# Last heads of a gated recurrence reordered, more MLP strips opened ahead, on one Trainium2 core

## The chip, the cores and the metric

The kernel runs on one core of a Trainium2 chip. The core has five engines that run side by side, each through a queue of its own in order: PE (TensorE, the matrix multiplier, with PEld for its weight loads), DVE (VectorE), ACT (ScalarE), POOL (GpSimd) and SP (SyncE, which here only issues DMAs). They wait for each other through semaphores. The metric is the device time of one execution in microseconds (us), as the median of several runs.

## The reference

A decoder trunk of two layers on one sequence of 1024 tokens, 1024 channels wide, everything in float32. Each layer is a token mixer followed by a gated MLP with a causal convolution over three tokens, each added to the residual stream. Layer 0's mixer is a gated linear recurrence (eight heads, 128 channels each), layer 1's is a multi-head latent attention. What matters here, cut:

```python
def _chunk_gated_recurrence(q, k, v, log_f):    # S_t = diag(f_t) S_{t-1} + k_t v_t^T ; o_t = S_t^T q_t
...
def _hgrn2_mixer(h, w_in, lower_bound, out_norm, w_out):
    q, f, i, g = jnp.split(h @ w_in, 4, axis=-1)
    ...
    forget = lb + (1.0 - lb) * jax.nn.sigmoid(f)
    o = _chunk_gated_recurrence(heads(jax.nn.silu(q)), heads(1.0 - forget), heads(i), heads(jnp.log(forget)))
    o = _rmsnorm(o, out_norm) * jax.nn.silu(heads(g))
    return o.reshape(B, S, D_MODEL) @ w_out

def _conv_ffn(h, w_up, conv_w, conv_b, w_down):
    u = h @ w_up                                # 1024 -> 2 * 2816
    y = conv_b + sum(u_pad[:, j:j + S, :] * conv_w[j] for j in range(3))
    gate, up = jnp.split(y, 2, axis=-1)
    return (jax.nn.silu(gate) * up) @ w_down
```

Both mixer and MLP read an RMS-normalised x (each token divided by the root of its mean square, then scaled per channel).

## The kernel before

The residual stream x stays on the chip as two halves of the sequence, `xt[0]` and `xt[1]`, each 128 partitions x 8 tiles x 512 tokens. A float32 product is made of three matmuls: each operand is split into a rounded part (`hi`, ACT's cast, L126) and its rest (`lo`, a subtraction on DVE or POOL, L129), and hi·hi + hi·lo + lo·hi is summed (L145 to L147, and `product`, L243, whose matmuls are recorded as L247). Weights come by SP's DMAs into a raw buffer and are split the same way (`load_w`; `whi`, `wlo`; three buffers each).

**The recurrence (layer 0).** A unit is one head on one half of the sequence. `project` (L333) makes its gate F, K, Q, v and g by 48 matmuls of 512 columns and 96 of 256; `recur` (L380) runs six levels of scores (`sc`, L388), each scaled on DVE (Q, L399) and POOL (K, L401) and folded into a score matrix `SD` (L392, L411), then the outputs `po` (L433, L435) and the state (L438, L443). The sum of squares of `po` for the head's norm is taken by four ACT squares whose elementwise result goes to a scrap tile `junk` (L447), followed by a chain of small DVE operations on `ss`, `oy`, `oz` (L450, L451) and the scaling of g (L453). `flip` (L457) transposes g and splits it (`oh`, `ol`), `wout` (L466) multiplies by the output weights and adds eight results into x (L299). The list `units` (L472) sets the order: head by head, first half then second, but the last four are (6,0), (7,0), (6,1), (7,1) as (head, half). While a unit's recurrence runs, the next unit's projection and the former unit's `wout` fill PE. The weights of a head are loaded when the head changes from one unit to the next (L499), so heads 6 and 7 are loaded twice.

**The MLP's up phase.** It works in 22 strips of 128 hidden channels for gate and up. Each strip is a 2x2 block product (halves of the inner dimension, halves of the sequence) done with seven products of 12 matmuls in place of eight (84 matmuls of 128x512). Its operands are block sums: `first_half` (L274) normalises `xt[0]` and splits it into two operands (`bop`), `second_half` (L278) normalises `xt[1]`, forms four differences (L285) and splits five more. `normalize` (L261) is: save x by a DMA, squares of the eight tiles on ACT with the sums on POOL (k below 4) and DVE (`token_scale`, L200 to L214), a matmul that sums over partitions (L165), an inverse root of twelve small DVE operations (L149), two diagonal matrices (`dg`, L189), a broadcast matmul (L197), an ACT copy `rb` (L219), and eight DVE operations that scale x in place (L266).

Two of the seven products need only the first half. `open_strips` (L250) does these two ahead for the strips in `OPENED` (L237: 1, 3, ... 15, eight of them): 24 matmuls each, copied out by ACT (`part`, L258) and saved by a DMA. In the strip loop (L924) an opened strip reads the saved part back and runs the other five products (60 matmuls); an unopened one runs all 84 there (`combos`, L832, makes the sums of its weights on DVE).

**What sets the order.** The tile framework gives every operation a priority by its place in the program, and orders each engine's queue by priority and by when operands come; code in `tc.high_priority()` goes ahead. On the chip each queue runs in that fixed order. `first_half` is written after the last unit's recurrence (L502), ahead of the last `wout`; `second_half` and `open_strips` follow, then the strips. Pools of one or two buffers (two `ps_mm` banks in PSUM, one `SD`, one `junk`) tie the queues together. Layer 1 uses the same `normalize`, `first_half`, `open_strips` and strips behind the attention.

Of the kernel before, what the change touches and what calls it, by code (L numbers as in the profile page):

```python
# [9 lines left out]
F32 = mybir.dt.float32  # L10
# [9 lines left out]
P = 128  # L20
D = 1024
# [5 lines left out]
NFF = DFF // P  # L27
# [31 lines left out]
def trunk_kernel(ctx: ExitStack, tc: tile.TileContext, x, pos, par, gout, cst, msk, w_hin, w_hout,  # L59
                 w_min, w_qup, w_kvup, w_mout, w_up, w_down, out):  # L60
    nc = tc.nc
    pe, dve, act, pool = nc.tensor, nc.vector, nc.scalar, nc.gpsimd
# [55 lines left out]
    rope_t = const.tile([P, 2, HF], F32, name="rope_t")  # L118

    def pcol(name, i):  # L120
        c = PC[name] + i
        return prm[:, c:c + 1]
# [46 lines left out]
    def token_rstd(groups, n, extra=None, tag="misc", name="st_y", vname="st_v"):  # L169
        sums = token_sums(groups, tag)  # L170
        w = 4 * len(groups)
        v = tpool.tile([P, w], F32, tag=vname, name="st_v", bufs=2 if vname == "st_v" else 1)
        y = tpool.tile([P, w], F32, tag=name, name="st_y", bufs=2 if name == "st_y" else 1)
        z = tpool.tile([P, w], F32, tag="st_z", name="st_z")
        if extra is None:
            dve.tensor_scalar(out=v, in0=sums, scalar1=1.0 / n, scalar2=EPS, op0=ALU.mult, op1=ALU.add)
        else:
            dve.scalar_tensor_tensor(out=v, in0=sums, scalar=1.0 / n, in1=extra, op0=ALU.mult, op1=ALU.add)
        rsqrt(v, y, z)
        return (y, v) if vname != "st_v" else y  # L180
# [12 lines left out]
    def bcast(y, tag="misc", lo_eng=pool):  # L193
        dg = diag(y, lo_eng)
        ps = ps_misc(tag)
        for i in range(2):
            pe.matmul(ps, lhsT=ones_r, rhs=dg[:, i].rearrange("p a b -> p (a b)"), start=(i == 0), stop=(i == 1))  # L197
        return ps

    def token_scale(hf):  # L200
        acc = tpool.tile([P, HF], F32, tag="acc", name="acc", bufs=1)
        acc2 = tpool.tile([P, 2 * HF], F32, tag="diag", name="acc2", bufs=1)[:, 0:HF]
        act.activation(out=acc2, in_=xt[hf][:, 0, :], func=AF.Square)
        for k in range(1, KD):
            if k == 4:
                act.activation(out=acc, in_=xt[hf][:, k, :], func=AF.Square)
                continue
            sq = tpool.tile([P, HF], F32, tag="sq", name="sq")
            act.activation(out=sq, in_=xt[hf][:, k, :], func=AF.Square)
            if k < 4:  # L210
                pool.tensor_tensor(out=acc2, in0=acc2, in1=sq, op=ALU.add)
            else:
                dve.tensor_tensor(out=acc, in0=acc, in1=sq, op=ALU.add)
        dve.tensor_tensor(out=acc, in0=acc, in1=acc2, op=ALU.add)  # L214
        return token_rstd([[acc]], D, name=f"y{hf}", vname=f"v{hf}")

    def spread_scale(hf, y, lo_eng=pool):
        rb = tpool.tile([P, HF], F32, tag=f"rb{hf}", name="rb", bufs=1)
        act.copy(out=rb, in_=bcast(y, lo_eng=lo_eng))  # L219
        return rb  # L220
# [13 lines left out]

    KH = KD // 2
    LO, HI = slice(0, KH), slice(KH, KD)
    OPENED = tuple(range(1, 17, 2))  # L237
    L, R = slice(0, HF), slice(HF, S)

    def halves(t):  # L240
        return [[x[:, i * HF:(i + 1) * HF] for x in t] for i in range(2)]
# [8 lines left out]
    def open_strips(layer, h):  # L250
        b11, b21 = h
        for j in OPENED:
            a11, a12 = halves(load_w(w_up[layer][j], eng=dve))
# [6 lines left out]

    def normalize(hf, layer):  # L261
        nc.sync.dma_start(out=xs[hf], in_=xt[hf])
        rb = spread_scale(hf, token_scale(hf)[0], dve)
        for k in (0, 4, 1, 5, 2, 6, 3, 7):
            xk = xt[hf][:, k, :]
            dve.scalar_tensor_tensor(out=xk, in0=xk, scalar=pcol("ffn", 8 * layer + k), in1=rb,  # L266
                                     op0=ALU.mult, op1=ALU.mult)
# [34 lines left out]
    def hgrn(layer, h):  # L302
        with ExitStack() as st:
            tp = st.enter_context(tc.tile_pool(name="g_t", bufs=2))
            early = st.enter_context(tc.tile_pool(name="g_e", bufs=2))
            wv = st.enter_context(tc.tile_pool(name="g_wv", bufs=1))
# [73 lines left out]
            def recur(hd, hf, prj, state):  # L380
                Fg, K, q, Q, v, g = prj
# [9 lines left out]
                SD = tp.tile([P, 4, 64], F32, tag="SD", name="SD", bufs=1)  # L391
# [35 lines left out]
                act.copy(out=kT, in_=pT)  # L427
                po = ps.tile([P, 4, P], F32, tag="o", name="po")
                ss = tp.tile([P, 4], F32, tag="ss", name="ss")
                junk = tp.tile([P, P], F32, tag="junk", name="junk", bufs=1)  # L430
                for c in range(4):
                    first = state is None
                    pe.matmul(po[:, c, :], lhsT=ST[:, c, :], rhs=v[:, c, :], start=True, stop=first)  # L433
                    if not first:
                        pe.matmul(po[:, c, :], lhsT=Q[:, c * P:(c + 1) * P], rhs=state, start=False, stop=True)  # L435
                    if not (hf == 1 and c == 3):
                        pu = ps.tile([P, P], F32, tag="sc", name="pu", bufs=2)
                        pe.matmul(pu, lhsT=kT[:, c, :], rhs=v[:, c, :], start=True, stop=True)  # L438
                        ns = tp.tile([P, P], F32, tag=f"state{hd % 2}", name="state")
                        if first:  # L440
                            act.copy(out=ns, in_=pu)
                        else:
                            dve.scalar_tensor_tensor(out=ns, in0=state, scalar=tot[:, c:c + 1], in1=pu,  # L443
                                                     op0=ALU.mult, op1=ALU.add)
                        state = ns
                for c in range(4):
                    act.activation(out=junk, in_=po[:, c, :], func=AF.Square, accum_out=ss[:, c:c + 1])  # L447
                y = tp.tile([P, 4], F32, tag="oy", name="oy")
# [21 lines left out]
                    add_x(hf, d, p)  # L470

            units = [(hd, hf) for hd in range(HEADS) for hf in range(2)]  # L472
            units[-3], units[-2] = units[-2], units[-3]
            vg_first = []
            for i, tag in enumerate(("hh1", "hl1")):
                raw = hpool.tile([P, 1024], F32, tag=tag, name="vgraw", padded_shape=[P, KD * HF])
# [1 line left out]
                vg_first.append(raw)  # L478
            weights(0)
            nc.sync.dma_start(out=xt[1], in_=x[1])  # L480
            goutb = wv.tile([P, P], F32, tag="goutb", name="goutb")
            nc.sync.dma_start(out=goutb, in_=gout.partition_broadcast(P))
            nc.sync.dma_start(out=cs, in_=cst)
            mstage = tp.tile([P, len(LEVELS), 64], F32, tag="ST", name="mstage", bufs=1)
# [3 lines left out]
            h.append(norm_x(1, "mix", layer))  # L488
            states, wos = {}, {}
            for i, (hd, hf) in enumerate(units):  # L490
                if hf == 0:
                    wos[hd] = load_w(w_hout[hd], "wo", wop, 2)
                late = [(pend[0], pend[1], *flip(pend[2]))] if i else []
                g, states[hd] = recur(hd, hf, prj, states.get(hd))
                for w in late:
                    wout(*w)
                pend = (hf, wos[hd], g)
                if i + 1 < len(units):
                    if units[i + 1][0] != hd:  # L499
                        weights(units[i + 1][0])  # L500
                    prj = project(*units[i + 1])
                if i + 1 == len(units):  # L502
                    h2 = first_half(layer)
            wout(pend[0], pend[1], *flip(pend[2]))
            return h2
# [320 lines left out]
    def up_phase(layer, h, wfp, ps_up):  # L826
        with ExitStack() as st:
# [44 lines left out]
            def strip(j, prev):  # L872
                opened = j in OPENED
                c = combos(j, opened)
# [178 lines left out]
```

## Time and profile before

| | |
|---|---|
| median of 3 runs | 2605.51 us (2604.63 to 2606.7) |
| the profiled execution | 2608.18 us, span 2606.4 us, mean granted TensorE clock 0.982 |
| busy share of the span | PE 95%, PEld 78%, DVE 69%, ACT 39%, POOL 19% |
| last unit pair of the recurrence, (6,1) and (7,1) | 605 to 654 us, the rest of the mixer to 684 us |
| opened strips of layer 0 and the wait at their end | 684 to 733.5 us |
| DMA | 228 MB, mean 88 GB/s |

The span is divided by stage: the recurrence takes the first 654 us, the up phase of layer 0 follows to about 1360 us with its down phase, the attention ends near 1920 us, and the second MLP fills the rest. A row of the timeline gives the start, the duration, the engine, the source line, the operation, what it writes from what it reads with the shapes, and in brackets how long the engine was idle ahead of it and what released it. `(x4110)` counts instructions.

### The profile page before, as it was taken

The page shows a single profiled execution, that of the slowest core. Times are in us where ns is not written, and L with a number is a line of the kernel's source. Part 1 is how long each engine was busy: PE and PEld are TensorE (multiplying, and loading weights), DVE is VectorE, ACT ScalarE, POOL GpSimd, SP SyncE. Part 2 cuts the span into 40 slices and gives each one's busy share as a digit, 9 for nine tenths or more (in the row PEclk, how much of TensorE's full clock was granted, in tenths as well). Part 3 has the DMA queues.
Part 4 walks back from the last instruction along what each step waited for, and adds up shares of the span by engine and source line. Part 5 has one row for each costly group of instructions (what it writes and reads, how often), then busy time and mean ns, then how long its engine had stood idle before and what let it go on. Part 6 is the DMA issues. An engine that isn't in the chain of part 4 may idle for free.

```text
span 2606.4 us, 35442 instructions
## 1 busy us (share of the span) xinstructions
PE 2474.9 (95%) x13732; PEld 2043.3 (78%) x13732; DVE 1795.3 (69%) x3218; ACT 1026.1 (39%) x1697; POOL 504.7 (19%) x489
## 2 busy tenths in 40 slices
PE   7999999998889999999999999999879999999999
PEld 6888888887667778888888777777757777888887
DVE  7455565667778888774545887877878888875333
ACT  4322222232444444433433444444434444443322
POOL 4343333543000000000013444443400000000000
PEclk9999999999999999999999899999989999999999
DMA  3011100211323232264431000000033332226443
GB/s 145 34 41 41 33 33 25 74 59 56 117 97 117 105 107 90 95 226 154 137 115 57 9 17 17 17 25 9 33 123 123 110 109 101 97 88 223 153 169 119
DMA packets 67561, 228.21 MB, mean 88 GB/s; under 512 B 7616, under 2 KB 8000, under 8 KB 66240
## 3 DMA queue, kind: packets, MB, share of 16 engines
q1 hardware_dynamic: 67392, 225.94, 24.5%
q8 instruction: 108, 1.77, 0.3%
q14 instruction: 61, 0.50, 0.1%
HBM read 181.87 MB, written 44.04 MB: 87 GB/s over the span
## 4 chain that ended last, share of the span: by engine, by line
PE 77%; DVE 16%; ACT 3%; issue 2%; DMA 1%; POOL 0%; ACTq 0%; DVEq 0%; SPq 0%; POOLq 0%
PE ps_mm L247 18%; PE ps_up L247 8%; PE ps_up L946 7%; PE ps_mm L145 6%; PE ps_mm L147 6%; PE ps_mm L146 6%; PE ps_mm L946 5%; PE ps_wo L946 4%; PE ps_wo L247 3%; PE sc L388 2%; PE ps_misc L946 2%; DVE x L299 2%; PE sp L701 2%; PE ps_wo L145 1%; DMA wraw<-in_w_up_dram 1%
## 5 line engine op out<-in xcount | busy, mean ns | idle before, releaser
L126 ACT CAST whi<-wraw 128x1024 fp32r<-128x1024 f32 (+1 forms) x312 | 304.9, 991 | 564.1 <-PE ps_misc L946 240.9
L247 PE MATMUL ps_mm<-bop,whi 128*128 128x512 f32 x1536 | 485.3, 398 | 40.2 <-ACT bop L126 15.8
L129 DVE TENSOR_TENSOR wlo<-wraw,whi 128x1024 fp32r<-128x1024 f32 (+1 forms) x266 | 299.5, 1139 | 286.0 <-ACT whi L126 282.6
L247 PEld LDWEIGHTS ps_mm<-bop,whi 128*128 128x128 f32 x1536 | 290.3, 191 | 115.2 <-ACT bop L126 16.3
L247 PE MATMUL ps_mm<-bop,wlo 128*128 128x512 f32 x768 | 299.7, 395 | 0.9 <-DVE wlo L129 0.9
L866 DVE SCALAR_TENSOR_TENSOR x<-x,prm,x 128x1023 f32<-128x1023 f32 (+1 forms) x176 | 223.6, 1280 | 50.5 <-ACT x L863 49.5
L247 PE MATMUL ps_up<-bop,whi 128*128 128x512 f32 x704 | 221.6, 395 | 0.4 <-ACT whi L126 0.4
L247 PEld LDWEIGHTS ps_mm<-bop,wlo 128*128 128x128 f32 x768 | 146.2, 190 | 33.6 <-DVE wlo L129 1.4
L946 PE MATMUL ps_up<-ring,whi 128*128 128x512 f32 x528 | 159.8, 389 | 0.0
L247 PEld LDWEIGHTS ps_up<-bop,whi 128*128 128x128 f32 x704 | 132.0, 188 | 32.5 <-ACT whi L126 2.0
L129 POOL TENSOR_TENSOR wlo<-wraw,whi 128x1024 fp32r<-128x1024 f32 x46 | 113.2, 2463 | 219.3 <-ACT whi L126 219.3
L145 PE MATMUL ps_mm<-vgh,hh 128*128 128x256 f32 x512 | 145.1, 284 | 5.4 <-DVE q L355 5.4
L147 PE MATMUL ps_mm<-vgh,hl 128*128 128x256 f32 x512 | 145.0, 283 | 0.0
L146 PE MATMUL ps_mm<-vgl,hh 128*128 128x256 f32 x512 | 143.7, 281 | 0.0
L247 PE MATMUL ps_up<-bop,wlo 128*128 128x512 f32 x352 | 138.5, 394 | 0.0
L399 DVE TENSOR_TENSOR Q<-Q,tot 128x256 f32<-128x256 f32 x96 | 63.0, 656 | 103.7 <-PE sc L388 79.8
L863 ACT ACTIVATE x<-x,prm 128x1024 f32<-128x1024 f32 x88 | 109.5, 1244 | 62.0 <-DVE x L890 38.3
L701 PE MATMUL sp<-kk,qq 128*128 128x384 f32 (+4 forms) x480 | 112.1, 363 | 16.6 <-ACT pp L716 13.5
L849 DVE TENSOR_TENSOR wraw<-wraw 128x512 f32<-128x512 f32 x176 | 121.0, 688 | 2.1
L145 PE MATMUL ps_mm<-hh,whi 128*128 128x512 f32 x288 | 115.6, 402 | 2.5 <-DVE g L375 1.6
L401 POOL TENSOR_TENSOR K<-K,tot 128x256 f32<-128x256 f32 x96 | 78.4, 816 | 192.8 <-PE sc L388 124.1
L946 PEld LDWEIGHTS ps_up<-ring,whi 128*128 128x128 f32 x528 | 99.1, 188 | 20.6
(302 smaller groups left out, 5689.6 us busy)
## 6 DMA issues: line engine op xcount, KB each, us to landing
wraw<-in_w_up_dram SPq DMA_DIRECT2D x104, 512.0 KB, 3.7
wraw<-in_w_down_dram SPq DMA_DIRECT2D x88, 512.0 KB, 3.5
act_spill<-x SPq DMA_DIRECT2D x44, 512.0 KB, 2.6
araw<-act_spill SPq DMA_DIRECT2D x88, 256.0 KB, 3.6
wraw<-in_w_hin_dram SPq DMA_DIRECT2D x38, 512.0 KB, 3.5
x_spill<-x SPq DMA_DIRECT2D x4, 2048.0 KB, 6.7
open_spill<-part SPq DMA_DIRECT2D x32, 256.0 KB, 2.3
x<-open_spill SPq DMA_DIRECT2D x16, 512.0 KB, 3.2
```

The costliest lines, as they stand in the source:

```text
L126: act.copy(out=hi, in_=src)
L129: lo_eng.tensor_tensor(out=lo, in0=src, in1=hi.bitcast(F32), op=ALU.subtract)
L145: pe.matmul(ps, lhsT=lh, rhs=rh, start=(i == 0), stop=False)
L146: pe.matmul(ps, lhsT=lh, rhs=rl, start=False, stop=False)
L147: pe.matmul(ps, lhsT=ll, rhs=rh, start=False, stop=(i == n - 1))
L247: pe.matmul(p, lhsT=a[l][:, ks], rhs=b[:, r, k, :], start=first and k == 0 and n == 0, stop=k == KH - 1 and n == 2, skip_group_check=not f ...
L401: pool.tensor_tensor(out=Kv[:, :, 0, :], in0=Kv[:, :, 0, :], in1=tv[:, :, 1:2].broadcast_to([P, nb, m]), op=ALU.mult)
L701: pe.matmul(sp[:, 0:n], lhsT=qq[:, a, qs], rhs=kk[:, c, cl], start=(i == 0), stop=last)
L849: dve.tensor_tensor(out=o, in0=p, in1=q, op=op)
L863: act.activation(out=y, in_=u, func=AF.Identity, scale=cw(2, ff), bias=pcol("cb", layer * 44 + ff))
L866: dve.scalar_tensor_tensor(out=y[:, i:S], in0=u[:, 0:S - i], scalar=cw(2 - i, ff), in1=y[:, i:S], op0=ALU.mult, op1=ALU.add)
L946: pe.matmul(acc[d], lhsT=w[l][:, d * P:(d + 1) * P], rhs=a[:, r], start=j == 0 and n == 0, stop=j == NFF - 1 and n == 2)
```

## The change

Five edits. (1) The last six units run as (5,0), (6,0), (7,0), (5,1), (6,1), (7,1), so heads 5, 6 and 7 are loaded twice, the state has three buffers, and the output weights are loaded again too. `first_half` is written after unit (5,1), two units ahead of the end. (2) `OPENED` holds 1, 3, ... 21: eleven strips. (3) In `normalize` the squares keep their priority, and everything from the partition sum to `rb` goes ahead in priority. (4) The scrap tile of the squares is no longer a tile of its own, but the front of `SD`. (5) `goutb` (the head norm's gain) lies in `rope_t`, which is filled only later.

```diff
-    def token_scale(hf):
+    def token_squares(hf):
...
-        return token_rstd([[acc]], D, name=f"y{hf}", vname=f"v{hf}")
+        return acc
+
+    def token_scale(hf):
+        return token_rstd([[token_squares(hf)]], D, name=f"y{hf}", vname=f"v{hf}")
...
-    OPENED = tuple(range(1, 17, 2))
+    OPENED = tuple(range(1, NFF, 2))
...
     def normalize(hf, layer):
         nc.sync.dma_start(out=xs[hf], in_=xt[hf])
-        rb = spread_scale(hf, token_scale(hf)[0], dve)
+        acc = token_squares(hf)
+        with tc.high_priority():
+            rb = spread_scale(hf, token_rstd([[acc]], D, name=f"y{hf}", vname=f"v{hf}")[0], dve)
...
-                junk = tp.tile([P, P], F32, tag="junk", name="junk", bufs=1)
+                junk = SD.rearrange("p a b -> p (a b)")[:, 0:P]
...
-                        ns = tp.tile([P, P], F32, tag=f"state{hd % 2}", name="state")
+                        ns = tp.tile([P, P], F32, tag=f"state{hd % 3}", name="state")
...
-            units[-3], units[-2] = units[-2], units[-3]
+            units = units[:-6] + sorted(units[-6:], key=lambda u: (u[1], u[0]))
...
-            goutb = wv.tile([P, P], F32, tag="goutb", name="goutb")
+            goutb = rope_t[:, 0, 0:P]
...
-                if hf == 0:
+                if hf == 0 or units[i - 1][0] != hd:
                     wos[hd] = load_w(w_hout[hd], "wo", wop, 2)
...
-                if i + 1 == len(units):
+                if (hd, hf) == units[-3]:
                     h2 = first_half(layer)
```

PE before, at the end of the recurrence: the last state and output matmuls of unit (7,1) (`pu`, `po`), then the first opened strips' products (`ps_mm<-bop`), and only after 24 of them the transposes of the last unit's g.

```order
L438 MATMUL pu<-v,K 128x128
L435 MATMUL po<-state,Q 128x128
L433 MATMUL po<-v,ST 128x128
L435 MATMUL po<-state,Q 128x128
L247 MATMUL ps_mm<-bop,whi 128x512 x3
L247 MATMUL ps_mm<-bop,wlo 128x512
L247 MATMUL ps_mm<-bop,whi 128x512 x2
```

PE now, at the same place: behind the last `po` come the transposes and the output product.

```order
L443 MATMUL pu<-v,K 128x128
L440 MATMUL po<-state,Q 128x128
L438 MATMUL po<-v,ST 128x128
L440 MATMUL po<-state,Q 128x128
L465 MATMUL ps_misc<-ident,g 128x128 x4
L145 MATMUL ps_wo<-oh,whi 128x512 x2
L146 MATMUL ps_wo<-ol,whi 128x512
L147 MATMUL ps_wo<-oh,wlo 128x512
```

PE now, inside unit (6,1): its scores (`sc`) stand among the broadcast of the row scale (`dg`) and the first opened products.

```order
L147 MATMUL ps_mm<-vgh,hl 128x256
L197 MATMUL ps_misc<-dg,ones_r 128x512
L393 MATMUL sc<-Q,K 64x64 x8
L197 MATMUL ps_misc<-dg,ones_r 128x512
L393 MATMUL sc<-Q,K 64x64 x16
L250 MATMUL ps_mm<-bop,whi 128x512 x3
L250 MATMUL ps_mm<-bop,wlo 128x512
```

The 48 opened products that stood behind the last `po` (two strips) now stand in unit (6,1); the order holds no others ahead of the end of the mixer, before or now.

DVE before, in unit (6,1): level by level the scaling of Q and the fold into SD, with the additions into x between.

```order
L399 TENSOR_TENSOR Q<-Q,tot_6118 128x64x4
L411 COPY_PREDICATED SD<-masks,sc 128x256
L375 SCALAR_TENSOR_TENSOR g<-ps_mm,st_y,g 128x128
L404 TENSOR_TENSOR tot_6525<-tot_6511 128x128
L129 TENSOR_TENSOR ol<-ps_misc,oh 128x512
L399 TENSOR_TENSOR Q<-Q,tot_6132 128x32x8
L411 COPY_PREDICATED SD<-masks,sc 128x256
```

DVE now, in the same unit, from the first use of the scrap in SD (`ss`, the former unit's squares) on.

```order
L455 TENSOR_SCALAR ss<-ss 128x4
L397 TENSOR_TENSOR SD<-sc,fold 128x256
L189 TENSOR_TENSOR dg<-ident,yl 128x512
L150 TENSOR_SCALAR oy<-ss 128x4
L416 COPY_PREDICATED SD<-masks,sc 128x256
L152 TENSOR_SCALAR oy<-oy 128x4
L129 TENSOR_TENSOR wlo<-wraw,whi 128x1024
L154 TENSOR_TENSOR oz<-oy 128x4
L380 SCALAR_TENSOR_TENSOR g<-ps_mm,st_y,g 128x128
L404 TENSOR_TENSOR Q<-Q,tot_6193 128x128x2
L416 COPY_PREDICATED SD<-masks,sc 128x256
L155 SCALAR_TENSOR_TENSOR oz<-oz,ss 128x4
```

Right behind these stand the eight scalings of x, and through the unit two splits of `bop` and three more of `wlo`. Where the squares go into SD, `ss` now stands ahead of the next unit's first write of SD; before, it stood some places behind it, in this unit and in the ones ahead.

## Rows read from the trace of the kernel before

**Rows 1.** The page's chain that ended last: share of the span by engine.

```profile
PE 77%; DVE 16%; ACT 3%; issue 2%; DMA 1%; POOL 0%; ACTq 0%; DVEq 0%; SPq 0%; POOLq 0%
```

**Rows 2.** Windows: from:to, length, busy us (count) by engine, clock, DMA share, GB/s.

```profile
100.00:605.00 505.00, 494.44 (x4110) 426.80 (x4108) 291.79 (x719) 135.62 (x349) 200.43 (x176) 1.00 0.13 43
605.00:630.00 25.00, 22.35 (x238) 18.36 (x238) 23.12 (x62) 11.74 (x32) 12.93 (x15) 1.00 0.13 53
630.00:654.20 24.20, 18.99 (x170) 15.09 (x169) 20.18 (x61) 4.41 (x14) 5.89 (x7) 0.86 0.08 34
654.20:684.00 29.80, 20.65 (x76) 14.73 (x76) 20.76 (x38) 13.34 (x22) 3.87 (x3) 0.89 0.15 53
684.00:733.50 49.50, 41.85 (x178) 33.70 (x178) 39.16 (x46) 24.11 (x29) 0.00 (x0) 0.93 0.42 160
733.50:767.00 33.50, 32.75 (x134) 26.13 (x135) 24.55 (x28) 14.65 (x18) 0.00 (x0) 0.95 0.31 101
972.70:1006.80 34.10, 33.42 (x146) 26.96 (x145) 29.13 (x34) 15.36 (x18) 0.00 (x0) 1.00 0.30 108
1044.90:1083.40 38.50, 38.50 (x169) 31.49 (x168) 29.48 (x33) 18.10 (x22) 0.00 (x0) 1.00 0.24 83
1921.40:1979.10 57.70, 55.33 (x230) 43.76 (x230) 46.64 (x52) 29.55 (x34) 0.00 (x0) 0.94 0.36 128
```

**Rows 3.** Timeline of PE from the last output matmul of the recurrence on.

```profile
653.64 0.49 PE L435 MATMUL po<-state,Q 128*128 128x128 f32 x2 [0.58 <-DVE state L443]
659.55 1.22 PE L247 MATMUL ps_mm<-bop,whi 128*128 128x512 f32 x2 [5.42 <-ACT bop L126]
668.57 0.60 PE L460 MATMUL ps_misc<-ident,g 128*128 128x128 f32 x4
674.25 0.63 PE L145 MATMUL ps_wo<-oh,whi 128*128 128x512 f32 x2
...
733.57 1.22 PE L247 MATMUL ps_mm<-bop,whi 128*128 128x512 f32 x2 [6.23 <-ACT whi L126]
```

**Rows 4.** Groups by line on DVE, 600 to 735: busy, mean ns, idle before.

```profile
L129 DVE TENSOR_TENSOR bop<-x,bop 128x2048 fp32r<-128x2048 f32 x6 | 13.7, 2289 | 0.0
...
L129 DVE TENSOR_TENSOR wlo<-wraw,whi 128x1024 fp32r<-128x1024 f32 x8 | 9.7, 1223 | 4.9 <-ACT whi L126 4.9
...
L213 DVE TENSOR_TENSOR acc<-acc,sq 128x512 f32<-128x512 f32 x6 | 4.5, 750 | 0.2 <-ACT sq L209 0.2
...
L189 DVE TENSOR_TENSOR dg<-ident,yl 128x512 fp32r<-128x512 f32 x2 | 1.4, 684 | 0.0
```

**Rows 5.** Timeline: the eight scalings of x alone, then beside POOL's additions.

```profile
700.99 5.39 DVE L266 SCALAR_TENSOR_TENSOR x<-x,prm,rb 128x512 f32<-128x512 f32 x8
...
1911.70 8.43 DVE L266 SCALAR_TENSOR_TENSOR x<-x,prm,rb 128x512 f32<-128x512 f32 x8 [1.21 <-ACT rb L219]
...
1912.33 4.60 POOL L211 TENSOR_TENSOR acc<-acc,sq 128x512 f32<-128x512 f32 x3 [14.34 <-ACT acc L203]
```

**Rows 6.** Timeline: DVE's SD and ss in (6,1), ss to ol in (7,1); ACT's last square.

```profile
605.73 0.42 DVE L392 TENSOR_TENSOR SD<-sc,fold 128x256 f32<-128x256 f32 x1 [0.53 <-PE sc L388]
...
609.47 0.16 DVE L450 TENSOR_SCALAR ss<-ss 128x4 f32<-128x4 f32 x1
...
631.92 0.17 DVE L450 TENSOR_SCALAR ss<-ss 128x4 f32<-128x4 f32 x1 [0.19 <-ACT junk L447]
...
638.48 0.69 DVE L129 TENSOR_TENSOR ol<-ps_misc,oh 128x512 fp32r<-128x512 f32 x1 [0.28 <-ACT oh L126]
...
655.73 0.19 ACT L447 ACTIVATION_READ_ACCUMULATOR junk<-po 128x1 f32 x1
```

**Rows 7.** Waits of PE by releaser, 802 to 870: total, times, longest.

```profile
PE ps_mm L247 <- ACT whi L126: 2.1, 2, 1.6
```

**Rows 8.** The same waits, 1979 to 2071.

```profile
PE ps_mm L247 <- ACT whi L126: 1.1, 1, 1.1
PE ps_mm L247 <- DVE wlo L129: 0.9, 1, 0.9
```

## The prediction, made before the changed kernel ran

> **What bounds the kernel now.** I read four views in this order. The chain of waits says which engine's work ends last: PE holds 77% of it and DVE 16% [rows 1], so the time is PE's work, and what can be won is PE's idle time. The windows then say where that lies. In the recurrence PE is busy 494.4 of 505 us: nothing to win there. In the stretch I call A, from the first scores of unit (6,1) to the finished second half of x (605 to 684), PE is busy 22.35 + 18.99 + 20.65 = 62.0 of 79.0 us, so 17 are idle, part of the rest runs at a lower granted clock (0.86 and 0.89), and DVE is busy 23.1 of the first 25 us. From 684 to 733.5 another 7.7 are idle. In the strip loop an opened and an unopened strip together take 34.1 us with PE idle for 0.7, while two unopened ones take 38.5 with no idle [rows 2]. The timeline of PE names the holes: 5.42 us ahead of the first opened product, and 6.23 us at 733.57, where the first strip of the loop waits for its weights [rows 3].
>
> **The change, part by part.** The sum is made against the profiled execution, 2608.18 us, which is 2.67 over the median of 2605.51; I carry the difference over to the median.
>
> *Stretch A, unit (6,1).* `first_half` now runs inside it. DVE gets eight scalings of x (5.4 us when alone [rows 5]), two `bop` splits (2 x 2.29), five weight splits `wlo` (5 x 1.22) and two `dg` (2 x 0.68), and loses four additions of squares (4 x 0.75, now in unit (5,1)) [rows 4]: 5.4 + 4.6 + 6.1 + 1.4 - 3.0 = +14.5. DVE had 25.0 - 23.1 = 1.9 idle there [rows 2], so the unit gets 12.6 longer. The order shows why the work can't slip aside: the scaling of Q for the next level, for which the next scores wait, stands behind each of these operations in DVE's queue. PE could do it in less: it gets 48 opened products, at 38.50 / 169 = 0.228 us each [rows 2] 10.9 us, onto 22.35, so 33.3 in all and +8.3. That is the lower bound.
>
> *Stretch A, POOL beside DVE.* Alone, the eight scalings took 5.39 us; beside 4.60 us of POOL additions they took 8.43 [rows 5], 0.66 us lost per us of POOL. POOL is busy 12.93 of 25 us in this unit [rows 2], about half. For the scalings alone that makes half of 3.0, +1.5; with nothing lost it is 0; and if all 17.5 added us lose by that rate, with POOL's 12.93 us spread over 37, it is 17.5 x 0.35 x 0.66 = +4.0. I take 1.5, since the scalings are what the rows show.
>
> *Stretch A, unit (7,1).* It loses the inverse root (twelve operations like `ss`, 0.17 each [rows 6], 2.0 us) and two `dg` (1.4), partly hidden: I take -2.0, between 0 and -3.4.
>
> *Stretch A, the tail.* Before, 48 opened products stand between the last `po` and the output product, and the whole tail takes 29.8 us [rows 2]. Now the chain is squares, inverse root, scaling, transposes, split, output product. Its price: in unit (7,1) the chain from `ss` to the end of `ol` took 639.2 - 631.9 = 7.3 us [rows 6], with that unit's own scalings of Q between; the squares ended at 655.9, 1.8 after the last `po` at 654.1 [rows 3, 6]; less some 1.5 for what stood between, 7.6. From the first output product to the end, 674.25 to 684.0, is 9.75 [rows 3]. Together 17.3, so -12.5; if the output product, too, is faster by the few us that the slow clock and the first `wlo` splits cost it, -14.5, and if PE's cold start costs more, -11.
>
> Sum of A: 12.6 + 1.5 - 2.0 - 12.5 = -0.4. What leaves the tail is bought back in unit (6,1).
>
> *Three more opened strips, layer 0.* The order has 48 opened products ahead of the end of A in both kernels. So what follows A grows by 3 x 24 = 72 products: 72 x 0.228 = +16.4. They cover the hole of 6.23 (-6.2), as ACT and DVE prepare the first strip of the loop beside them. DVE has three more `wlo` splits (3.7 us) ahead of it: +1.2 as a guess between 0 and 3.7. Without that hole the granted clock needn't fall to 0.95 for the 33.5 us behind it: -1.7 [rows 2]. Then three pairs of unopened strips become mixed pairs: 3 x (34.1 - 38.5) = -13.2. Note that 24 products cost 5.5 in front and give back only 4.4, since a mixed pair isn't as dense. The waits of 2.1 for `whi` early in the loop [rows 7] go, as ACT is ahead: -2.1. Sum: -5.6, from -8 (no `wlo` delay, mixed pairs packed as dense as the rest) to +1 (the hole stays).
>
> *The same in layer 1.* There is no such hole: PE is busy 55.3 of 57.7 us among the opened strips [rows 2], of which I fill half, -1.2. So 16.4 - 1.2 - 13.2, less the waits of 1.1 and 0.9 [rows 8], plus 1.2 for `wlo` again, +1.2; from -1 to +4. The order of the row-scale chain at the end of the attention doesn't change, so the priority edit does nothing there.
>
> *The recurrence ahead of A.* Head 5 is loaded a second time and three output weights too: four and three times a split of ACT and POOL. POOL is busy 200 of 505 us and ACT 136 [rows 2], so they hide; were they not covered, POOL's queue would delay a scaling of K. Squares into `SD`: the next unit's first write of SD now stands behind the former unit's squares. SD started at 605.73 and `ss` at 609.47 [rows 6], so it comes up to 3.7 us later, and the fourth and later groups of scores behind it. What hides it is PE's queue: two groups of scores and then a run of the next unit's projection, dozens of matmuls, ahead of the third group. I take +1.5 for all units together, from 0 to +6.
>
> **Sum:** -0.4 - 5.6 + 1.2 + 1.5 = -3.3. From 2608.18 that gives 2604.9, and by the median 2605.51 - 3.3 = 2602.2; I say 2602.
>
> **The rivals.**
>
> R1, *PE, not DVE, sets unit (6,1)*: its cost is 8.3 in place of 12.6, since DVE's small operations fall into gaps and PE's opened products cover the waits for scores. For it: in unit (6,1) PE is idle for 2.7 us, and the products stand among the scores, where it waits. Against: 23.1 of 25 us busy on DVE. Time: 2602.2 - 4.3 = 2598.
>
> R2, slower: *each unit's recurrence waits for the former unit's squares.* 14 units hand SD on. If PE runs out of projection before the delayed scores come, it idles in each; at 1 us of the 3.7 that is +14 in place of +1.5: 2614.7. It decides the sign from (3.3 + 1.5) / 14 = 0.34 us per unit. For it: `ss` now stands ahead of SD in DVE's queue in every unit. Against: the projection between the second and third group of scores.
>
> R3, *the hole at 733.57 stays*, because DVE's three more splits delay the same weights: +6.2 and the clock's +1.7: 2602.2 + 7.9 = 2610.1. For it: DVE is busy 39.2 of 49.5 us there [rows 2], so it has little to catch up with. Against: what ends the hole is ACT's `whi`, and ACT is busy 24.1.
>
> R4, *DVE and POOL shut each other out in unit (6,1)*: were each us of POOL in that unit lost to the 17.5 us of added two-input operations at their share of the time, 12.93 / 37 = 0.35, it is +6.1 in place of +1.5: 2602.2 + 4.6 = 2606.8. The row at 1911.70 shows 3.0 lost to 4.60 us of POOL, so less than all. This rival is the rule of the Trainium skill, page "SBUF — State Buffer", section "Who interferes with whom": a DVE operation with two inputs in SBUF and a GpSimd operation that reads SBUF exclude each other for the whole instruction. By that rule the scalings would have lost 4.6 us; the trace bears out two thirds of it.
>
> **How the numbers follow.** This measurement can tell about 0.2%, 5.2 us: faster is below 2600.3, slower above 2610.7. My forecast has 0.42, with a range of its own from 2594 to 2610: of that 0.18 faster, 0.20 same, 0.04 slower. R1 has 0.23: 0.19 faster, 0.04 same. R2 has 0.17: 0.15 slower, 0.02 same. R3 has 0.06: 0.03 same, 0.03 slower. R4 has 0.12: 0.02 faster, 0.06 same, 0.04 slower. Together faster 0.39, same 0.35, slower 0.26. The range for 8 in 10 takes in R1, R3 and R4 and most of R2: 2592 to 2613.
>
> **What would show it.** Right: the first scores of unit (6,1) still near 605 to 607, the unit some 37 us long with DVE busy nearly all of it; no opened product behind the last `po`, the tail near 17 us; no hole at the start of the strip loop; three more mixed pairs at 34 us. R1: the unit near 33 us and PE dense in it. R2: PE idle ahead of the third group of scores in every unit, waiting for DVE's SD or Q, and the last units starting 10 us later. R4: scalings of x at over 1 us each in unit (6,1). The forecast is wrong if the start of unit (6,1) moves by more than 6 us, or if the opened strips in front take over 20 us more.

## The result, and the profile after

The changed kernel is slower: 2638.29 us (median of 4 runs, 2635.32 to 2640.07) against 2606.11 us, a ratio on record of 1.0117 with a 95% interval of 1.0105 to 1.0129 (the two medians alone give 1.0123). The forecast was 2602 with a range to 2613. The profiled execution took 2637.33 us, with a span of 2635.6.

The windows of the changed kernel by stage (columns as in [rows 2]): the recurrence up to the first scores of unit (6,1), then (6,1), (7,1), the tail, the stretch from the finished second half of x to the first convolution in two pieces, and a mixed pair of strips.

```profile
100.00:621.40 521.40, 501.79 (x4100) 430.11 (x4099) 300.58 (x723) 143.57 (x360) 216.91 (x183) 0.99 0.14 48
621.40:669.20 47.80, 36.18 (x272) 29.18 (x271) 38.29 (x81) 17.47 (x34) 12.66 (x11) 0.82 0.21 67
669.20:694.30 25.10, 18.34 (x177) 14.88 (x177) 17.68 (x43) 4.77 (x14) 8.84 (x9) 0.80 0.07 22
694.30:711.20 16.90, 10.23 (x33) 5.86 (x32) 10.37 (x28) 6.60 (x16) 3.86 (x3) 0.80 0.00 1
712.75:778.00 65.25, 62.44 (x274) 50.16 (x273) 44.81 (x51) 31.25 (x38) 0.00 (x0) 1.00 0.50 179
778.00:790.60 12.60, 11.48 (x47) 8.78 (x48) 7.56 (x9) 5.37 (x6) 0.00 (x0) 1.00 0.27 83
927.20:961.30 34.10, 33.42 (x146) 26.96 (x145) 29.13 (x35) 15.30 (x17) 0.00 (x0) 1.00 0.31 108
```

The same two units of the kernel before, cut at their first scores as above:

```profile
605.00:629.20 24.20, 21.55 (x223) 17.63 (x222) 22.88 (x61) 11.74 (x32) 12.62 (x14) 1.00 0.11 44
629.20:654.20 25.00, 19.79 (x187) 15.82 (x186) 20.41 (x62) 4.41 (x14) 6.20 (x8) 0.86 0.11 43
```

Set side by side, the 29.2 us between the two spans divide so: unit (6,1) starts 16.4 later (621.4 against 605.0); it takes 47.8 in place of 24.2, +23.6; unit (7,1) +0.1; the tail 16.9 in place of 29.8, -12.9; all that follows (2635.6 - 711.2 against 2606.4 - 684.0) +2.0. The forecast for these five was +1.5, +14.1, -2.0, -12.5 and -4.4, so of the 32.5 us by which it missed, 14.9 lie ahead of unit (6,1), 9.5 in it, 2.1 in (7,1) and 6.4 behind the mixer; the tail came out 0.4 better.

In unit (6,1) PE is idle for 11.6 of 47.8 us and its granted clock averages 0.82, against 2.7 of 24.2 and 1.00. PE's timeline there shows three holes:

```profile
632.52 0.85 PE L393 MATMUL sc<-Q,K 128*64 128x64 f32 x16 [2.28 <-DVE Q L404]
639.64 1.12 PE L393 MATMUL sc<-Q,K 128*64 128x64 f32 x16 [6.26 <-DVE Q L404]
644.69 0.79 PE L250 MATMUL ps_mm<-bop,whi 128*128 128x512 f32 x1 [2.78 <-DVE bop L129]
...
651.68 0.57 PE L393 MATMUL sc<-Q,K 128*64 128x64 f32 x12
```

and DVE's timeline what stood in front of them, and what DVE waited for afterwards:

```profile
632.71 5.79 DVE L271 SCALAR_TENSOR_TENSOR x<-x,prm,rb 128x512 f32<-128x512 f32 x8
...
639.08 0.41 DVE L404 TENSOR_TENSOR Q<-Q,tot 128x256 f32<-128x256 f32 x1
...
653.15 0.43 DVE L404 TENSOR_TENSOR Q<-Q,tot 128x256 f32<-128x256 f32 x1 [3.60 <-PE sc L393]
```

The eight scalings of x run in one piece from 632.71 to 638.5. The scaling of Q, for which the next scores wait, stands behind them in DVE's queue, so PE idles 6.26 us. Then PE waits 2.78 for `bop`, and runs opened products from 644.69 to 651.68 while the next scores stand behind these in PE's queue: now DVE idles 3.60 us. The scalings took 5.79 against 5.39 alone [rows 5]; POOL was busy for only 1.12 us beside them.

In the tail no opened product stands ahead of the transposes any more, as forecast (compare [rows 3]). The hole of 6.23 us at the first strip of the loop is gone, and the longest wait for `whi` near it is 0.89; a wait of 1.83 for the copy of a partial sum is new:

```profile
699.71 1.25 PE L465 MATMUL ps_misc<-ident,g 128*128 128x128 f32 x4 [4.61 <-DVE g L458]
...
752.97 0.73 PE L250 MATMUL ps_mm<-bop,whi 128*128 128x512 f32 x2 [1.83 <-ACT part L261]
...
781.92 0.73 PE L250 MATMUL ps_mm<-bop,whi 128*128 128x512 f32 x2 [0.89 <-ACT whi L126]
```

Inside the recurrence SD is written when the former unit's squares are done. In the unit whose first scores ran at 418.01, DVE's rows are:

```profile
422.42 0.16 DVE L455 TENSOR_SCALAR ss<-ss 128x4 f32<-128x4 f32 x1
422.49 0.41 DVE L397 TENSOR_TENSOR SD<-sc,fold 128x256 f32<-128x256 f32 x1
```

SD comes 4.5 us after the first scores; in the kernel before 0.73 (605.73 against 605.00, [rows 6]). PE does not wait there. But the later levels of scores stand later in its queue (the last one runs 34.1 us behind the first scores, 29.0 in the kernel before), so at the unit's end there is nothing left to put between its last, short matmuls. The end of that unit, PE, changed kernel:

```profile
452.12 0.68 PE L419 MATMUL sc<-Q,K 128*64 128x64 f32 x8
453.26 0.49 PE L438 MATMUL po<-v,ST 128*128 128x128 f32 x2 [0.46 <-ACT ST L425]
...
455.36 0.71 PE L443 MATMUL pu<-v,K 128*128 128x128 f32 x4 [0.73 <-ACT K L432]
456.29 0.49 PE L440 MATMUL po<-state,Q 128*128 128x128 f32 x2 [0.22 <-DVE state L448]
...
457.60 0.69 PE L393 MATMUL sc<-q,K 128*64 128x64 f32 x16
```

and the same place in the kernel before, where products of `wout` and of the next projection stand between:

```profile
438.91 0.68 PE L414 MATMUL sc<-Q,K 128*64 128x64 f32 x8
...
443.81 0.48 PE L145 MATMUL ps_wo<-oh,whi 128*128 128x512 f32 x1
...
445.29 0.28 PE L146 MATMUL ps_mm<-vgl,hh 128*128 128x256 f32 x1
...
446.23 0.61 PE L438 MATMUL pu<-v,K 128*128 128x128 f32 x4
...
448.37 0.69 PE L388 MATMUL sc<-q,K 128*64 128x64 f32 x16
```

This unit is 39.59 us long in the changed kernel (418.01 to 457.60) and 38.43 before (409.94 to 448.37). About half of the 1.16 is the scrap's: with the scrap apart (next section) the unit takes 38.98.

### The profile page after: what moved, and what is told of

It reads as the page before. It is cut to its first block, busy times and chain, and to the rows that moved or that the text cites. A ratio compares the mean times of both kernels' runs of the same rounds, so it can differ in the third digit from the quotient of the medians.

```text
span 2635.6 us, 35560 instructions
## 1 busy us (share of the span) xinstructions
PE 2484.9 (94%) x13732; PEld 2045.4 (78%) x13732; DVE 1814.4 (69%) x3230; ACT 1028.9 (39%) x1692; POOL 523.6 (20%) x496
## 4 chain that ended last, share of the span: by engine, by line
PE 58%; DVE 11%; ACT 2%; DMA 1%; issue 1%; POOL 0%; SPq 0%; ACTq 0%; DVEq 0%; POOLq 0%
PE ps_mm L250 19%; PE ps_up L250 8%; PE ps_up L951 7%; PE ps_mm L951 4%; PE ps_wo L951 4%; PE ps_misc L951 2%; PE ps_wo L250 2%; DVE x L304 2%; PE ps_mm L145 2%; PE sp L706 2%; PE ps_mm L147 2%; PE ps_mm L146 1%; PE ps_misc L165 1%; DMA wraw<-in_w_up_dram 1%; DVE mx L711 1%
## 5 line engine op out<-in xcount | busy, mean ns | idle before, releaser
L250 PE MATMUL ps_mm<-bop,whi 128*128 128x512 f32 x1584 | 500.6, 397 | 38.2 <-ACT x L897 13.5
L250 PEld LDWEIGHTS ps_mm<-bop,whi 128*128 128x128 f32 x1584 | 296.8, 189 | 118.7 <-ACT x L897 22.9
L250 PE MATMUL ps_mm<-bop,wlo 128*128 128x512 f32 x792 | 308.2, 393 | 0.0
L871 DVE SCALAR_TENSOR_TENSOR x<-x,prm,x 128x1023 f32<-128x1023 f32 (+1 forms) x176 | 222.5, 1280 | 18.2 <-ACT x L868 16.9
L129 POOL TENSOR_TENSOR wlo<-wraw,whi 128x1024 fp32r<-128x1024 f32 x51 | 125.0, 2454 | 230.0 <-ACT whi L126 222.0
```

The costliest lines, as they stand in the source:

```text
L129: lo_eng.tensor_tensor(out=lo, in0=src, in1=hi.bitcast(F32), op=ALU.subtract)
L250: pe.matmul(p, lhsT=a[l][:, ks], rhs=b[:, r, k, :], start=first and k == 0 and n == 0, stop=k == KH - 1 and n == 2, skip_group_check=not f ...
L871: dve.scalar_tensor_tensor(out=y[:, i:S], in0=u[:, 0:S - i], scalar=cw(2 - i, ff), in1=y[:, i:S], op0=ALU.mult, op1=ALU.add)
```

## The experiments

Theory S: the squares in SD delay every unit. Theory E: `first_half` inside a unit makes DVE's and PE's queues hold each other up, and the clock falls behind the idle time. The rivals are W or U (the second loading of head 5 and the order of units), and the prediction's own sum. Ratios are those on record, to the kernel before, run beside, with 95% intervals.

**Scrap of the squares apart** (the changed kernel otherwise).

```diff
-                junk = SD.rearrange("p a b -> p (a b)")[:, 0:P]
+                junk = rope_t[:, 1, 0:P]
```

> The changed kernel, but the scrap of the squares goes to an unused part of rope_t instead of the front of SD. Theory S (squares in SD delay every unit): of the 22.4 us by which unit (6,1) starts later, 14 to 18 go, the rest (weights of head 5 again, 4 to 8 us) stays; unit (6,1) stays long (40 to 47 us); time about 2638 - 16 = 2622, between 2618 and 2625. Rival W (the second loading of head 5's weights and the new order of units cost the 22 us): unit (6,1) still starts near 628, time 2635 to 2640.

Measured 2634.69, ratio 1.0102 (1.0089 to 1.0115). Up to the tenth unit the pace of the kernel before is back, but unit (6,1) still starts at 615.4, +10.4, and takes 48.4. The time is outside theory S's range and just below rival W's, and the start is neither's. Taking the scrap away gained about 4, not 16, and the two intervals overlap; unit (6,1) starts 6.0 earlier by it. The other parts of the change cost 27 without it.

**Scrap in SD, alone** (the kernel before with this edit).

```diff
-                junk = tp.tile([P, P], F32, tag="junk", name="junk", bufs=1)
+                junk = SD.rearrange("p a b -> p (a b)")[:, 0:P]
```

> The kernel before with one edit alone: the scrap of the squares goes to the front of SD. Theory S: each unit's levels of scores come later, PE's projection is used up before the unit's end; the last units start 14 to 20 us later, time 2620 to 2626. Rival W: no change, 2604 to 2608.

2624.61, ratio 1.0063 (1.0051 to 1.0075): +16 to +17, as theory S says, with runs from 2617 to 2628. Unit (6,1) starts at 621.3. That this edit costs 16 alone and about 4 on top of the rest shows that the two delays before unit (6,1) don't add: part of the overlap is in unit (5,1), which takes 42.7 in the changed kernel and 46.0 with the scrap apart.

**Eight strips in place of eleven** (scrap apart), and **eleven in place of eight** (the kernel before).

```diff
-    OPENED = tuple(range(1, NFF, 2))
+    OPENED = tuple(range(1, 17, 2))
```

> The changed kernel with the scrap apart and eight opened strips in place of eleven. By the prediction's terms the three more strips are worth -5.6 in layer 0 and +1.2 in layer 1, so this kernel would be 4.4 slower than the one with the scrap apart and eleven. If the strips are worth nothing or cost (the stretch behind the mixer grew by 2 us in the changed kernel), it is 0 to 4 faster.

> The kernel before with eleven opened strips alone. By the prediction's terms -4.4: 2601.5. If the hole at 733.57 isn't filled, or the opened products run no denser, +2 to +6: 2608 to 2612.

Eight: 2629.32, ratio 1.008 (1.0067 to 1.0093), 5.4 faster than eleven, more than either reading allowed. Eleven in the kernel before: 2611.46, ratio 1.0015 (1.0007 to 1.0024), +3.6, where the prediction's terms gave -4.4. The three strips cost 3.6 to 5.4 us. The windows from the last sum of squares to the first convolution, kernel before and then the one with eleven, show where:

```profile
685.50:749.30 63.80, 56.63 (x235) 45.13 (x235) 46.69 (x54) 29.57 (x34) 0.00 (x0) 0.92 0.37 136
```

```profile
684.30:763.80 79.50, 75.61 (x322) 60.12 (x322) 52.38 (x60) 36.78 (x44) 0.00 (x0) 0.98 0.46 160
```

PE's idle time falls from 7.2 to 3.9, not by 6.2. Its busy time rises by 19.0 for 87 matmuls more (x235 to x322), 0.22 each, so a product costs no more than forecast; 72 of the 87 are the three strips', and the other 15 are the loop's own, which stand ahead of the first convolution here. Cut where 84 products of the loop are done, the same work in both, the front grows by 12.4, where the sum had +9.7, and the rest of the loop gives back 12.0 and not 15.3. The waits of 2.1 for `whi` early in the loop [rows 7], which were to go, are still there with eleven strips (PE's waits from 761 to 1128):

```profile
PE ps_mm L247 <- ACT whi L126: 2.1, 2, 1.6
```

In layer 1, cut in the same way, the front costs 15.1 and the loop gives back 10.4.

**first_half last again** (scrap apart), and **the order of units alone** (this, with eight strips and without the raised priority).

```diff
-                if (hd, hf) == units[-3]:
+                if i + 1 == len(units):
```

> The changed kernel with the scrap apart and first_half back behind the last unit; the new order of the units, head 5's second loading and eleven strips stay. Theory E (first_half inside a unit costs, since its operations and the opened products stand in DVE's and PE's queues between the levels of scores, and the two engines wait for each other): unit (6,1) back at 24 to 26 us, the time 2611 (eleven strips alone) plus 2 to 5 for head 5's loading: 2612 to 2617. Rival U (the order of units and the loading cost it): unit (6,1) stays over 40 us, 2630 to 2636.

> The new order of the last six units with head 5 loaded twice, and nothing else of the change: scrap apart, eight strips, no raised priority, first_half written behind the last unit. If the second loading of head 5 is what delays unit (6,1) (POOL's weight splits, the queue ahead of it), unit (5,1) is 5 to 7 us longer than the 38.6 of before and the whole +6 to +12: 2613 to 2619. If the delay comes from first_half's squares alone, unit (5,1) stays at 39 to 40 and the time within 4 us of before.

2622.41, ratio 1.0056 (1.0038 to 1.0073), with runs from 2616 to 2626; and 2618.32, ratio 1.0036 (1.0023 to 1.0049). The first of these times lies between theory E's 2617 and rival U's 2630. Of the 21 us of eight strips with the scrap apart, the order of units carries about 9, and the early `first_half` with the raised priority the other 12. Unit (6,1) is back at 28.0 to 28.1, near theory E. But as x's first half is now done one unit earlier, the scheduler itself pulls most of `first_half` into (7,1), which takes 37 to 38 in place of 25, and its squares into (5,1). Windows of units (5,1), (6,1) and (7,1) with the order alone:

```profile
569.38:613.19 43.81, 38.27 (x317) 32.45 (x316) 31.32 (x62) 15.98 (x37) 24.33 (x19) 1.00 0.28 97
613.19:641.24 28.05, 25.49 (x223) 20.95 (x222) 24.23 (x60) 11.24 (x28) 8.86 (x12) 0.82 0.23 76
641.24:679.38 38.14, 29.76 (x210) 23.77 (x210) 29.73 (x69) 8.71 (x17) 7.82 (x9) 0.78 0.06 21
```

Unit (5,1) is 5.2 longer than the 38.6 of the unit in its place in the kernel before, (7,0). PE idles 5.5 of its 43.8 us. The longest wait, 2.50, is for a state update that stands on DVE behind two additions of squares; these take 3.44 in place of some 1.5 while POOL splits a weight beside them (rows of DVE, POOL and PE):

```profile
607.40 3.44 DVE L213 TENSOR_TENSOR acc<-acc,sq 128x512 f32<-128x512 f32 x2
```

```profile
607.49 2.80 POOL L129 TENSOR_TENSOR wlo<-wraw,whi 128x1024 fp32r<-128x1024 f32 x1 [1.23 <-ACT whi L126]
```

```profile
611.88 0.49 PE L438 MATMUL po<-state,Q 128*128 128x128 f32 x2 [2.50 <-DVE state L446]
```

**Weight splits for (6,1) on DVE** (first_half last).

```diff
-            def weights(hd):
+            def weights(hd, eng=pool):
...
-                        weights(units[i + 1][0])
+                        weights(units[i + 1][0], dve if i == 13 else pool)
```

> The kernel with first_half written last (new order of units, scrap apart, eleven strips), with the weight splits for unit (6,1) on DVE in place of POOL. If POOL's four weight splits, beside the squares' additions, are what make unit (5,1) 6 us longer, it gets 3 to 6 shorter, 2616 to 2619. If DVE's queue is as full, no change, 2620 to 2624.

2620.24, ratio 1.0048 (1.0031 to 1.0065); unit (5,1) 44.5 against 44.6. It doesn't tell: POOL's busy time in that unit is 24.27 as before, so the splits that I moved did not stand in it. On DVE they run from 532 to 553, in unit (7,0), which takes 38.9 in place of 40.9. How (5,1)'s extra time divides between POOL's splits and the squares of `first_half` stays open; the rows above show the two meeting.

**No raised priority** (scrap apart).

```diff
-        acc = token_squares(hf)
-        with tc.high_priority():
-            rb = spread_scale(hf, token_rstd([[acc]], D, name=f"y{hf}", vname=f"v{hf}")[0], dve)
+        rb = spread_scale(hf, token_scale(hf)[0], dve)
```

> The changed kernel with the scrap apart and without the raised priority of the row-scale chain. If the raised priority is what puts the chain's matmuls in front of PE's queue in unit (5,1) (a wait of 2.2 us for the sum of squares), unit (6,1) starts 2 to 5 us earlier and the time is 2629 to 2633. If it does nothing, 2632 to 2637.

2630.24, ratio 1.0089 (1.0074 to 1.0104); with it 1.0102 (1.0089 to 1.0115). Unit (6,1) starts at 614.2 in place of 615.4. The intervals overlap: unclear, and small either way.

**first_half one unit later** (scrap apart), and **one unit earlier in the kernel before**.

```diff
-                if (hd, hf) == units[-3]:
+                if (hd, hf) == units[-2]:
```

```diff
-                if i + 1 == len(units):
+                if i + 2 == len(units):
```

> The changed kernel with the scrap apart and first_half one unit later, behind (6,1), so that it falls into (7,1), which has no projection of a next unit. Theory E: the same levels of scores are drawn apart, but the opened products now fill the waits of a unit in which PE is idle anyway: (6,1) at 24 to 26 us, (7,1) 40 to 45 in place of 25, the tail short as now; 2615 to 2625. If only the total of DVE's work counts, as the prediction had it, (7,1) gets about 14 longer and the tail 12.5 shorter: 2612 to 2618.

> The kernel before, with first_half one unit earlier (behind (6,1) in place of (7,1)) and nothing else: eight strips, the old order of units. Theory E: (7,1) gets 15 to 20 us longer and the tail 12 to 13 shorter, +3 to +8: 2611 to 2616. By the prediction's sum it is about even, 2605 to 2609.

2629.94, ratio 1.0084 (1.0067 to 1.0101), slower than either expectation: units (6,1) and (7,1) take 33.2 and 36.4, so the work spreads over both. And 2611.16, ratio 1.0019 (1.0009 to 1.0028), +3.9, as theory E has it. The last is the cleanest trial of moving `first_half` inside; windows of (7,1) and the tail:

```profile
628.20:670.31 42.11, 34.08 (x235) 26.22 (x234) 31.17 (x71) 11.24 (x20) 5.91 (x8) 0.80 0.13 51
670.31:688.27 17.96, 10.43 (x29) 6.49 (x30) 11.18 (x28) 7.67 (x19) 3.86 (x3) 0.81 0.15 54
```

(7,1) grows by 17.1 and the tail shrinks by some 13.

**One scaling of x in place of eight**, and **no strip opened in layer 0** (both with the scrap apart).

```diff
-        for k in (0, 4, 1, 5, 2, 6, 3, 7):
+        for k in (0, 4, 1, 5, 2, 6, 3, 7) if hf or layer else (0,):
```

```diff
-        for j in OPENED:
+        for j in OPENED * layer:
...
-                opened = j in OPENED
+                opened = j in OPENED * layer
```

> The changed kernel with the scrap apart, leaving out seven of the eight scalings of the first half of x in layer 0. By the sum of DVE's work unit (6,1) gets 7 x 0.68 = 4.7 us shorter: 43 to 44 in place of 48.4. By theory E the scalings hold up the scores, PE stands idle 6 us behind them and its granted clock falls: without them the idle time goes and the clock stays up, 8 to 14 us shorter: 34 to 40.

> The changed kernel with the scrap apart and no strip of layer 0 opened ahead (layer 1 has its eleven), so that only the first unopened strip's 24 products on the first half can come into unit (6,1). By theory E, opened products standing in PE's queue ahead of the next scores hold DVE up: with half of them unit (6,1) is 5 to 9 us shorter than 48.4. If DVE's own work sets the unit (36 us of it in 48), only the three weight splits less count, 3 to 4 us shorter. The time as a whole isn't told by it: without opened strips PE idles behind the mixer.

Windows of units (5,1) and (6,1) with the scrap apart, then with one scaling, and of (6,1) with none opened:

```profile
569.37:615.39 46.02, 40.90 (x325) 34.98 (x324) 32.15 (x69) 16.48 (x37) 24.27 (x19) 0.96 0.30 104
615.39:663.77 48.38, 37.83 (x267) 31.31 (x266) 36.77 (x79) 17.25 (x33) 9.30 (x11) 0.79 0.23 66
```

```profile
568.14:615.42 47.28, 41.63 (x325) 35.57 (x324) 34.39 (x74) 18.29 (x39) 24.20 (x19) 0.94 0.29 101
615.42:650.70 35.28, 33.35 (x270) 27.06 (x270) 30.47 (x68) 15.37 (x32) 9.31 (x11) 0.98 0.28 90
```

```profile
613.80:651.45 37.65, 28.47 (x238) 23.48 (x237) 33.25 (x77) 13.14 (x28) 10.89 (x12) 0.83 0.00 1
```

Without seven scalings, 4.7 us of DVE's time, unit (6,1) is 13.1 shorter: PE's idle time falls from 10.6 to 1.9, its clock averages 0.98, and 4.5 us of its busy time go with that. One split of `bop`, which then waits for no scaling, moves up into (5,1), so the two units are to be taken together: 11.8 shorter for 4.1 us less of DVE's work, nearly three times as much. Without opened strips 12 of the 48 products are left in the unit, not half of them, and one of the five weight splits. The unit is 10.7 shorter, though DVE's work falls by only 3.5: the other 7.2 are DVE's idle time. The hole of 6.24 us behind the scalings stays, and the clock averages 0.83:

```profile
632.56 1.12 PE L393 MATMUL sc<-Q,K 128*64 128x64 f32 x16 [6.24 <-DVE Q L404]
```

The 36 products that are gone had taken 9.1 us of PE's time, so here the gain is not much more than PE's own work. Both trials show the same: the unit's length is not the sum of DVE's work but what the two queues cost each other. Times as a whole: 2620.74, ratio 1.0046 (1.0031 to 1.0061), against 2634.69 with all scalings; and 2636.1, ratio 1.0103 (1.0088 to 1.0118).

**first_half behind the last output product** (the kernel before), with eight and with eleven strips.

```diff
-                if i + 1 == len(units):
-                    h2 = first_half(layer)
             wout(pend[0], pend[1], *flip(pend[2]))
+            h2 = first_half(layer)
             return h2
```

> The kernel before with first_half written behind the last wout, so the other way from the change: nothing of it stands in a unit or ahead of the last output product. The tail falls from 31 to 18 us, as in the changed kernel, without a unit being drawn out; the 48 opened products (11 us) and two splits (4.6 us on DVE) come behind it. If they cover the hole of 6.2 us: 2600 to 2606. If DVE's later start only moves the wait to the front of the strip loop: 2607 to 2614.

> The same with eleven opened strips. If DVE's later start leaves a hole in front of the loop, the three more strips fill it, 0 to 5 us faster than with eight; if not, they cost 3 to 5 as in the kernel before.

2606.71, ratio 0.9998 (0.9989 to 1.0007), and 2613.2, ratio 1.0024 (1.0014 to 1.0033). With eight strips nothing is lost and nothing won, between the two readings; the three more strips cost 6.5 here. The output product runs early, but PE then idles for `bop`:

```profile
680.01 1.22 PE L247 MATMUL ps_mm<-bop,whi 128*128 128x512 f32 x2 [9.93 <-ACT bop L126]
```

**Six opened strips in layer 1** (the kernel before).

```diff
-        for j in OPENED:
+        for j in OPENED[:len(OPENED) - 2 * layer]:
...
-                opened = j in OPENED
+                opened = j in OPENED[:len(OPENED) - 2 * layer]
```

> The kernel before with six opened strips in layer 1 (eight in layer 0). With eleven strips layer 1 was 4.5 us slower, 1.5 per strip; if that holds downwards, two strips fewer give -3: 2605 against 2608. If the opened products cover the second half's preparation in layer 1, a hole opens in front of the strip loop: 2610 to 2616.

2615.52, ratio 1.0035 (1.0022 to 1.0047). PE's waits by releaser from 1920 to 2080 show the hole:

```profile
PE ps_mm L247 <- ACT whi L126: 10.1, 2, 8.9
```

In layer 1 eight strips cover the preparation of the second half: six open a hole, and eleven only cost; no number between was run. No version was faster than the kernel before beyond its interval.

## Why the prediction was wrong, point by point

- *Unit (6,1), +12.6 by DVE's work, with +1.5 for POOL*: one of the two steps that failed, and the one to learn from; it missed by 9.5 us. DVE's work was right (forecast 22.9 + 14.5 = 37.4 us, measured 38.3), but the sum took it for the unit's length, as if DVE never waited. DVE idled 9.5 of 47.8 us and PE 11.6, in turns: the scores behind the scalings, then the scalings of Q behind the opened products. PE's granted clock averaged 0.82 there, and the 48 opened products took 14.9 us in place of 10.9. Shown by one scaling (-11.8 over two units for 4.1 us of DVE's work) and by none opened (-10.7 for 3.5). The prediction saw DVE's queue, where the scaling of Q stands behind each added operation, but not PE's, where the next scores stand behind the opened products. R1, that PE fills the gaps and the unit gets 33, was further off still. The +1.5 for POOL was about right in size, if not in place: the scalings lost 0.4, and two of the five weight splits, beside POOL, took 1.9 in place of 1.22. R4's 6.1 did not come; as POOL was mostly idle during the scalings, this is no test of its rule.
- *The recurrence ahead, +1.5*: measured +16.4, the other step that failed and the larger miss, 14.9. Part of it is rival R2, given 0.17. Alone its edit makes unit (6,1) start 16.3 later, 1.2 us per unit, so R2's price of 14 was near; in the changed kernel 6.0 of the 16.4 go when the scrap is apart, so that the total comes near R2's is in part luck. And its mechanism was not quite the one described: PE doesn't idle ahead of the third scores. The levels of scores move back in PE's order, the projection is used up, and the short matmuls at the unit's end stand bare. I looked for cover at the place of the delay, and it was missing at the end of the unit. The other part, 10.4 with the scrap apart, was priced as hidden or not at all: the order of units with head 5's second loading, and the additions of squares, which the sum took out of (6,1) at -3.0 and charged to (5,1) at nothing. Unit (5,1) is 5.2 longer with the order alone, where the squares stand in it too; what each of the two costs stays open.
- *Unit (7,1), -2.0*: +0.1. It lost the inverse root as said, but its clock averaged 0.80, 0.86 before, and its `ss` and SD waited for the squares.
- *The tail, -12.5*: -12.9. Right.
- *Layer 0's strips, -5.6*: from the last sum of squares to the last convolution, +0.4 with eleven strips alone and -3.9 in the changed kernel. The price of a product was right. PE's idle time in front shrank by 3.3 and not by 6.2, and the loop gave back 12.0 and not 15.3 (eleven strips alone).
- *Layer 1's strips, +1.2*: +4.7 with eleven strips alone, +4.4 in the changed kernel. The front cost 15.1, less than the 16.4 of the sum, but the loop gave back 10.4 and not 15.2.

## What to carry to other kernels

When work is moved into a stretch where two engines hand results to and fro step by step, don't add its duration to the busier engine: look in both queues at which hand-over stands behind it, since each such block idles the other engine and may lower the clock of what follows. A shared buffer that makes one step later can cost at the far end of a unit, where the filling work has run out, so look for the cover along the whole unit. And work done ahead pays only as far as it fills a hole: in layer 1 eight opened strips filled it, six left one, and eleven cost.

## What the runs showed of the hardware that was not expected

A DVE operation on 128x4 elements took 1.98 us, against 0.17 [rows 6], where a subtraction on POOL ran beside it. POOL's row and DVE's row in the changed kernel:

```profile
672.71 2.33 POOL L129 TENSOR_TENSOR wlo<-wraw,whi 128x1024 fp32r<-128x1024 f32 x1
```

```profile
673.09 1.98 DVE L455 TENSOR_SCALAR ss<-ss 128x4 f32<-128x4 f32 x1 [1.04 <-ACT SD L452]
```

Both end at about 675.05, so DVE's operation, which has a single input, seems to have waited for POOL's to end. The other traces bear it out. In the first 720 us of all seventeen, 41 operations of this form on DVE (`TENSOR_SCALAR` on 128x4) stood beside a two-input operation of POOL with more than 0.25 us to go: all 41 took over 0.5 us, up to 2.2, and ended within 0.04 us of POOL's. Of 963 with no POOL operation so beside them none took over 0.25.

The means of the granted clock, 0.82 in unit (6,1) and 0.80 behind it, are a switching between two levels, full and half. The changed kernel's windows, cut where it switches:

```profile
632.90:650.00 17.10, 8.06 (x42) 5.91 (x38) 16.50 (x30) 4.90 (x4) 4.23 (x3) 0.50 0.16 54
650.00:673.80 23.80, 21.27 (x161) 16.82 (x159) 12.63 (x25) 7.68 (x18) 4.66 (x6) 1.00 0.21 67
673.80:684.10 10.30, 6.36 (x70) 5.28 (x71) 8.66 (x27) 0.59 (x1) 4.58 (x5) 0.50 0.16 52
```

It fell at 632.9, during the one group of scores between PE's holes of 2.28 and 6.26 us, and rose at 650.0, when PE had run opened products without a wait from 644.69 on. With one scaling in place of eight it averaged 0.98 in unit (6,1), and the 48 products took 12.0 us in place of 14.9.
